# Hybrid attention block on one core: roots, low parts and transposes of the first norm moved, weights of the last norm moved

## Chip, core and metric

The kernel runs on one core of one Trainium2 chip. The core has TensorE (PE in the profile), VectorE (DVE), ScalarE (ACT), GpSimd (POOL) and the SyncE queue (SP), which here issues all transfers. The metric is the device time of one launch in microseconds.

## What is computed

The input x is 1024 x 1024 in float32. With `rms(v, g) = v * rsqrt(mean(v*v) + 1e-6) * g` the block is

```python
h = rms(x, pre_norm_mix)
proj = h @ w_in                        # 1024 x 3280
o_a = sparse_attention(proj, ...)      # scores, top 256 keys of each row, softmax over latents
o_b = gated_delta_rule(proj, ...)      # convolution, chunks of 64, triangular inverses
x = x + rms(concat(o_a, o_b) @ w_out, post_norm_mix)
h = rms(x, pre_norm_mlp)
y = square(relu(h @ w_mlp_in)) @ w_mlp_out
out = x + rms(y, post_norm_mlp)
```

Only the first norm (top line) and the last one (bottom line) are touched by the change, and the first loads of `w_in`.

## The kernel before

Large products are made from split operands: a float32 matrix is written as a high part, rounded to fp32r, and a low part, the difference. `mm3` (L199 to L201) then issues three matmuls: high x high, low x high, high x low.

**Start.** 34 matmuls on zeros run on PE while the eight 128-row tiles of x are loaded. The rows are worked on in two halves of four tiles. For each half ScalarE squares the tiles and sums them (L312), VectorE makes the factor 1/sqrt of four columns in `rsqrt` (L313, then by shifting the bits of the number and three refining steps of three instructions, L212 to L217) and scales the four tiles (L317). Then come eight blocks k of 128 columns: PE transposes four 128 x 128 pieces into one PSUM bank (L321), ScalarE writes the high part `hTH` with the norm's weight as scale (L323), VectorE the low part `hTL` (L324). The bank comes from `pst()`, a pool `tr` of two banks. `psx()` hands out banks of `tr` and of a second pool of two, `ch`, in turn.

**Columns of w_in.** `fetch(i)` loads the i-th group of columns of `plan` into `stg`, ScalarE (for i under 7) or GpSimd casts it to the high part `wh` (L266, L268), and GpSimd subtracts for the low part `wl` (L269). Group 0 has 80 columns (keys of the indexer, gates), groups 1 to 4 have 128 (queries of the indexer). The products go into a PSUM tile `two` that holds both halves of the rows; the second half of group 0 is written only when VectorE has read the first half (L383 to L385).

**Middle.** Scores of the indexer (L471 to L479), a bitwise search for the 256th largest score on VectorE and ScalarE (L521 to L533), convolutions (L587 to L592), chunked recurrences, attention, output product and the two MLP products.

**End.** For each of eight row blocks PE adds a last stretch of w_mlp_out to two banks (24 matmuls), VectorE adds the banks to the sum in SBUF (L1776), and `finish` makes the last norm: ScalarE squares and sums (L1272), VectorE and ScalarE make the factor (`rsqrt` with `act=True`: L209 is a square root from ScalarE's table, L210 its reciprocal, and L215 to L217 one refining step), GpSimd multiplies the sum by the norm's weights (L1763, two halves of 512 columns), VectorE multiplies by the factor and adds x (L1764), SyncE stores.

The order of instructions on each engine is set when the program is built: a scheduler with its own cost model merges the streams. Each engine then works off its list in that order and waits on semaphores.

Of the kernel before, what the change touches and what calls it, by code (L numbers as in the profile page):

```python
# [8 lines left out]
F32 = mybir.dt.float32  # L9
# [4 lines left out]
OP = mybir.AluOpType  # L14
# [125 lines left out]
def block_kernel(ctx: ExitStack, tc: tile.TileContext, x, w_in, c_norm, w_uk, w_uv, rel_bias, conv_w, a_log,  # L140
# [4 lines left out]
    V, S, G, PE, SY = nc.vector, nc.scalar, nc.gpsimd, nc.tensor, nc.sync  # L145
# [4 lines left out]
    w_in, c_norm, w_uk, w_uv, conv_w, a_log = w_in[0], c_norm[0], w_uk[0], w_uv[0], conv_w[0], a_log[0]  # L150
# [22 lines left out]
    def psw():  # L173
        return pl.t(ps_w, [P, T], F32, "two")

    def pst():
        return pl.t(ps_t, [P, 512], F32, "tr")

    def psc():
        return pl.t(ps_c, [P, 512], F32, "ch")  # L180

    def pss():
        return pl.t(ps_s, [P, 512], F32, "sc")
# [3 lines left out]
    def psx():  # L187

        turns[0] += 1
        return (pst, psc)[turns[0] % 2]()  # L190
# [12 lines left out]
    def rsqrt(pool, a, n, tag, y=None, act=False):  # L203


        y = pl.t(pool, [P, n], F32, tag + "_y", bufs=4) if y is None else y
        u = pl.t(pool, [P, n], F32, tag + "_u", bufs=4)
        if act:
            S.activation(y, a, AF.Sqrt)  # L209
            V.reciprocal(y, y)  # L210
        else:
            V.tensor_scalar(u.bitcast(I32), a.bitcast(I32), 1, None, op0=OP.logical_shift_right)  # L212
            V.tensor_scalar(y.bitcast(I32), u.bitcast(I32), -1.0, float(0x5F3759DF), op0=OP.mult, op1=OP.add)
        for _ in range(1 if act else 3):
            V.scalar_tensor_tensor(u, y, -0.5, y, op0=OP.mult, op1=OP.mult)  # L215
            V.tensor_mul(u, u, a)
            V.scalar_tensor_tensor(y, u, 1.5, y, op0=OP.add, op1=OP.mult)  # L217
        return y

    def paired(t):  # L220

        return t.rearrange("p (b a) -> p a b", a=2)

    def halves(t):
        return t.rearrange("p (a b) -> p a b", a=2)
# [26 lines left out]
    hTH = pl.t(hp_, [P, NK, T], F32R, "hTH")  # L252
    hTL = pl.t(hp_, [P, NK, T], F32R, "hTL")

    def load_cols(cols, w=w_in, act=True, stage=None):

        n = sum(c for _, c in cols)
        wh = pl.t(wp, [P, NK, P], F32R, "wh")
        wl = pl.t(wp, [P, NK, P], F32R, "wl")
        f = pl.t(stage, [P, NK, P], F32, "stg", bufs=2) if stage else pl.t(stg, [P, NK, P], F32, "stg")  # L260
        at = 0
        for c0, c in cols:
            SY.dma_start(f[:, :, at:at + c], w[:, c0:c0 + c].rearrange("(k p) c -> p k c", p=P))
            at += c
        if act:
            S.copy(wh[:, :, :n], f[:, :, :n])  # L266
        else:
            G.tensor_scalar(wh[:, :, :n], f[:, :, :n], 1.0, 1.0, op0=OP.mult, op1=OP.mult)  # L268
        G.tensor_sub(wl[:, :, :n], f[:, :, :n], wh[:, :, :n].bitcast(F32))  # L269
        return wh, wl, n  # L270

    plan = [("kw", 0)] + [("qi", p) for p in range(4)] + [(n, h) for h in range(4) for n in ("kb", "qb")]
# [2 lines left out]
    loaded = {}  # L275

    def fetch(i):
        if i < len(plan) and i not in loaded:
            kind, p = plan[i]
            cols = [(C_KI, 72), (C_AB, 8)] if kind == "kw" else [(first[kind] + P * p, P)]  # L280
            loaded[i] = load_cols(cols, act=i < 7)

    kq, kq_close = pl.open("kq", side="right")
    px, px_close = pl.open("px", side="right")
# [3 lines left out]
    ps = psw()  # L288
# [3 lines left out]
    for tb in range(NB):  # L292
        xt = pl.t(px, [P, D], F32, f"x{tb}")
        r0 = tb // 4 * 512 + tb % 2 * 256 + tb % 4 // 2
        SY.dma_start(xt, x[r0:r0 + 255:2, :])
        xs.append(xt)
        if tb == 3:
            sv = pl.t(px, [66, P], F32, "sv")
            SY.dma_start(sv[0:48, :], conv_w.rearrange("j (b p) -> (j b) p", p=P))
            SY.dma_start(sv[48:56, :], pre_norm_mix.rearrange("(k p) -> k p", p=P))  # L300
            SY.dma_start(sv[56:57, :], o_norm[None, :])
            SY.dma_start(sv[57:65, :], pre_norm_mlp.rearrange("(k p) -> k p", p=P))
            fetch(0)
    ps = pst()
# [3 lines left out]
    for half in range(2):  # L308
        ss = pl.t(px, [P, 4], F32, f"ss{half}")
        for j in range(4):  # L310
            junk = pl.t(px, [P, D], F32, "junk", bufs=2)
            S.activation(junk, xs[half * 4 + j], AF.Square, accum_out=ss[:, j:j + 1])  # L312
        V.tensor_scalar(ss, ss, 1.0 / D, EPS, op0=OP.mult, op1=OP.add)  # L313
        rs = rsqrt(px, ss, 4, f"rs{half}")
        for j in range(4):
            xt = xs[half * 4 + j]
            V.tensor_scalar(xt, xt, rs[:, j:j + 1], None, op0=OP.mult)  # L317
        for k in range(NK):
            ps = pst()
            for j in range(4):  # L320
                PE.transpose(ps[:, j * P:(j + 1) * P], xs[half * 4 + j][:, k * P:(k + 1) * P], ident)  # L321
            sl = slice(half * 512, half * 512 + 512)
            S.activation(hTH[:, k, sl], ps, AF.Identity, scale=svT[:, 48 + k:49 + k])  # L323
            V.scalar_tensor_tensor(hTL[:, k, sl], ps, svT[:, 48 + k:49 + k], hTH[:, k, sl].bitcast(F32),  # L324
                                   op0=OP.mult, op1=OP.subtract)
# [626 lines left out]
    def projections():  # L952
        nonlocal dna, dn, dn_close
        for i, (kind, p) in enumerate(plan):
            for j in range(1, 3):
                fetch(i + j)
# [293 lines left out]
    gain = c_row.rearrange("p n c -> p (n c)")  # L1250
    r2 = pl.t(keep, [P, NB], F32, "r2")
    pool, wo, h2, early = {}, [], {}, []
# [14 lines left out]
    def sumsq(ps, pool, out=None, bufs=3, act=False):  # L1267

        s2 = pl.t(pool, [P, 2], F32, "s2", bufs=4)
        for c in range(2):  # L1270
            junk = pl.t(pool, [P, 512], BF16, "jk", bufs=bufs)
            S.activation(junk, ps[c], AF.Square, accum_out=s2[:, c:c + 1])  # L1272
        v = pl.t(pool, [P, 1], F32, "v", bufs=4)
        V.tensor_scalar(v, s2[:, 0:1], s2[:, 1:2], 1.0 / D, op0=OP.add, op1=OP.mult)
        V.tensor_scalar(v, v, EPS, None, op0=OP.add)
        return rsqrt(pool, v, 1, "rm", out, act)
# [90 lines left out]
    stage, x1 = {}, {}  # L1367
# [96 lines left out]
    def tmp(dtype=F32):  # L1464
        return pl.t(tmpp, [P, 512], dtype, "tmp2")
# [109 lines left out]
    while ready:  # L1575
# [4 lines left out]
        ps = bank_[{2: 1, 3: 5, 4: 7}.get(j, j)]  # L1580
# [138 lines left out]
    while ready:  # L1719
# [4 lines left out]
        c, j, ops = ready.pop(0)  # L1724
# [3 lines left out]
        for t in range(4):  # L1728
            ps = bank_[set_][t]
# [11 lines left out]
    for f in range(NS):  # L1741
# [5 lines left out]
        w = []  # L1747
# [5 lines left out]
    def finish(tb, yt):  # L1753
        xr = pl.t(stg, [P, D], F32, "stg")

        r0 = tb // 4 * 512 + tb % 4 * 64
        for a in range(2):
            SY.dma_start(xr[a::2, :], x1_d[r0 + 256 * a:r0 + 256 * a + 64, :])
        r = sumsq(yt, fin, bufs=1, act=True)
        for c in range(2):  # L1760
            cs = slice(c * 512, c * 512 + 512)
            yg = tmp()
            G.tensor_tensor(halves(yg), paired(yt[c]), halves(gain[:, cs]), OP.mult)  # L1763
            V.scalar_tensor_tensor(xr[:, cs], yg, r, xr[:, cs], op0=OP.mult, op1=OP.add)  # L1764
            for a in range(2):
                SY.dma_start(out[r0 + 256 * a:r0 + 256 * a + 64, cs], xr[a::2, cs])


    for tb in range(NB):
        yt = [acc[n][:, tb % 4] for n in (("11", "12"), ("21", "22"))[tb // 4]]  # L1770
        for c in range(2):
            ps = psc() if c else pss()
            for f, (hq, w) in enumerate(rows):
                ts_ = slice(tb * P, (tb + 1) * P)
                mm3(ps, hq[:, 0, ts_], hq[:, 1, ts_], w[c][0], w[c][1], f == 0, f == NS - 1, True)
            V.tensor_add(yt[c], yt[c], ps)  # L1776
        finish(tb, yt)
# [28 lines left out]
```

## Time and profile before

| | |
|---|---|
| runs (us) | 1382.74, 1387.98, 5743.25; median 1387.98 |
| profiled execution | 1387.9 us, of which the span from first to last instruction is 1386.2 |
| granted TensorE clock, mean | 0.965 of full |
| busy share of the span | PE 93%, DVE 80%, ACT 53%, POOL 18% |

The profile counts an engine as busy while it executes; a row of the timeline has its start, its duration, the instruction and, in brackets, how long the engine sat idle before it and what it waited for.

### The profile page before, as it was taken

The page shows a single profiled execution, that of the slowest core. Times are in us where ns is not written, and L with a number is a line of the kernel's source. Part 1 is how long each engine was busy: PE and PEld are TensorE (multiplying, and loading weights), DVE is VectorE, ACT ScalarE, POOL GpSimd, SP SyncE. Part 2 cuts the span into 40 slices and gives each one's busy share as a digit, 9 for nine tenths or more (in the row PEclk, how much of TensorE's full clock was granted, in tenths as well). Part 3 has the DMA queues.
Part 4 walks back from the last instruction along what each step waited for, and adds up shares of the span by engine and source line. Part 5 has one row for each costly group of instructions (what it writes and reads, how often), then busy time and mean ns, then how long its engine had stood idle before and what let it go on. Part 6 is the DMA issues. An engine that isn't in the chain of part 4 may idle for free.

```text
span 1386.2 us, 20222 instructions
## 1 busy us (share of the span) xinstructions
PE 1284.0 (93%) x6628; PEld 1110.4 (80%) x6628; DVE 1108.2 (80%) x2552; ACT 735.4 (53%) x1543; POOL 253.7 (18%) x276
## 2 busy tenths in 40 slices
PE   7899999888777999998989899999999899999995
PEld 4578888777666999877878788888887788888885
DVE  5555779999998888987677467888777987888886
ACT  5455457676624777776455456566666333333422
POOL 3112322122233444348020000000000000000023
PEclk8999999999987999999999899999999999999998
DMA  6223224445055332324355916655566975746215
GB/s 195 66 88 106 61 77 122 137 140 134 23 142 155 97 114 81 93 86 162 125 180 185 298 67 213 213 204 196 208 213 239 392 259 203 251 120 206 77 52 176
DMA packets 184146, 213.33 MB, mean 154 GB/s; under 512 B 28161, under 2 KB 123626, under 8 KB 183914
## 3 DMA queue, kind: packets, MB, share of 16 engines
q1 hardware_dynamic: 184042, 212.06, 47.2%
q8 instruction: 52, 0.85, 0.2%
q14 instruction: 52, 0.43, 0.1%
HBM read 138.58 MB, written 75.00 MB: 154 GB/s over the span
## 4 chain that ended last, share of the span: by engine, by line
PE 65%; DVE 19%; DMA 7%; ACT 5%; issue 2%; POOL 0%; SPq 0%; DVEq 0%; ACTq 0%
PE sc L199 4%; PE sc L200 4%; PE sc L201 4%; PE ch L201 4%; PE ch L199 4%; PE ch L200 4%; PE acc L199 4%; PE acc L200 4%; PE acc L201 4%; DVE pre L528 3%; PE two L199 3%; PE two L200 3%; PE two L201 3%; PE tr L199 2%; PE tr L201 2%
## 5 line engine op out<-in xcount | busy, mean ns | idle before, releaser
L199 PE MATMUL two<-hTH,wh 128*128 128x512 f32 (+1 forms) x416 | 164.5, 398 | 23.0 <-ACT tmp L409 10.6
L200 PE MATMUL two<-hTL,wh 128*128 128x512 f32 (+1 forms) x416 | 163.9, 394 | 0.0
L201 PE MATMUL two<-hTH,wl 128*128 128x512 f32 (+1 forms) x416 | 162.0, 391 | 0.0
L1763 POOL TENSOR_TENSOR tmp<-acc,c_row 128x512 f32<-128x512 f32 x16 | 20.7, 1301 | 644.1 <-DVE acc L1776 632.5
L521 ACT ACTIVATE jk<-score,cand 128x1024 bf16<-128x1024 f32 (+2 forms) x96 | 92.4, 964 | 46.8 <-DVE cand L533 36.2
L199 PEld LDWEIGHTS two<-hTH,wh 128*128 128x128 f32 (+1 forms) x416 | 80.6, 194 | 38.9 <-issue 19.7
L200 PEld LDWEIGHTS two<-hTL,wh 128*128 128x128 f32 (+1 forms) x416 | 80.8, 194 | 11.7 <-issue 0.5
L201 PEld LDWEIGHTS two<-hTH,wl 128*128 128x128 f32 (+1 forms) x416 | 80.1, 193 | 12.0 <-issue 0.5
L1426 ACT CAST hl<-raw 128x512 fp32r<-128x512 f32 x81 | 48.6, 614 | 71.4 <-PE acc L200 51.5
L269 POOL TENSOR_TENSOR wl<-stg,wh 128x1024 fp32r<-128x1024 f32 (+1 forms) x26 | 61.1, 2351 | 80.7 <-ACT wh L266 79.3
L1426 ACT CAST hl<-tt 128x512 fp32r<-128x512 f32 x56 | 34.4, 616 | 72.9 <-PE tr L200 44.6
L1426 ACT CAST hl<-tmp 128x512 fp32r<-128x512 f32 x60 | 35.8, 617 | 55.9 <-DVE tmp L1543 30.6
L1427 DVE TENSOR_TENSOR hl<-raw,hl 128x512 fp32r<-128x512 f32 x81 | 55.2, 684 | 4.5 <-ACT hl L1426 3.3
L1187 ACT CAST part<-tr 128x512 fp32r<-128x512 f32 x80 | 42.7, 542 | 27.3 <-PE tr L1185 24.0
L1162 ACT ACTIVATE big<-big,nm 128x256 f32<-128x256 f32 (+6 forms) x64 | 50.4, 789 | 11.3 <-DVE nm L1161 9.4
L1188 DVE TENSOR_TENSOR part<-tr,part 128x512 fp32r<-128x512 f32 x80 | 50.0, 629 | 4.3 <-ACT part L1187 4.0
L1210 PE MATMUL acc<-part,VS 128*128 128x256 f32 x288 | 51.7, 303 | 0.7 <-DVE part L1188 0.7
L268 POOL TENSOR_SCALAR wh<-stg 128x1024 fp32r<-128x1024 f32 x19 | 19.9, 1049 | 174.8 <-PE two L200 160.6
L589 DVE SCALAR_TENSOR_TENSOR tmp<-two,svT,tmp 128x1023 f32<-128x1023 f32 (+2 forms) x36 | 45.9, 1276 | 6.1 <-ACT tmp L587 6.0
L1138 POOL TENSOR_TENSOR mt<-tz,maskb 128x256 f32<-128x256 f32 x56 | 37.6, 681 | 59.3 <-DVE mx L1154 46.2
L199 PE MATMUL acc<-h2H,hl 128*128 128x512 f32 x120 | 46.3, 387 | 1.6 <-ACT tmp L1477 1.6
L1185 PE MATMUL tr<-ident,big 128*128 128x128 f32 x288 | 46.7, 277 | 0.5 <-DVE part L1188 0.4
(507 smaller groups left out, 4121.7 us busy)
## 6 DMA issues: line engine op xcount, KB each, us to landing
hid<-tmp SPq DMA_DIRECT2D x140, 256.0 KB, 2.6
hq<-hid SPq DMA_DIRECT2D x80, 256.0 KB, 5.3
raw<-in_w_mlp_in_dram SPq DMA_DIRECT2D x14, 1024.0 KB, 5.5
tmp<-hid SPq DMA_DIRECT2D x56, 256.0 KB, 5.4
raw<-in_w_mlp_out_dram SPq DMA_DIRECT2D x13, 1024.0 KB, 7.4
stg<-in_w_in_dram SPq DMA_DIRECT2D x25, 512.0 KB, 4.3
x<-in_x_dram SPq DMA_DIRECT2D x8, 512.0 KB, 5.3
la_d<-la SPq DMA_DIRECT2D x8, 512.0 KB
```

What stands on the lines that cost most here:

```text
L199: PE.matmul(o, lh, rh, start=start, stop=False, skip_group_check=more)
L200: PE.matmul(o, lh, rl, start=False, stop=False, skip_group_check=more)
L201: PE.matmul(o, ll, rh, start=False, stop=stop, skip_group_check=more)
L269: G.tensor_sub(wl[:, :, :n], f[:, :, :n], wh[:, :, :n].bitcast(F32))
L521: S.activation(junk[:, :n], s_of(b), AF.Sign, bias=cand[:, 3 + i:4 + i].bitcast(F32), scale=-1.0, accum_out=cnt[:, 3 + i:4 + i])
L589: V.scalar_tensor_tensor(acc[:, 3 - j:T], both[:, 0:T - 3 + j], w[j], acc[:, 3 - j:T], op0=OP.mult, op1=OP.add)
L1162: S.activation(pr[:, :n], pr[:, :n], AF.Exp, bias=nm, accum_out=den[:, hh:hh + 1])
L1185: PE.transpose(ps[:, c * P:(c + 1) * P], u["p"][hh][:, (j + a) * P:(j + a + 1) * P], ident)
L1188: V.tensor_sub(pt[:, 0:2 * nj, 1, :], v4(ps)[:, 0:2 * nj], pt[:, 0:2 * nj, 0, :].bitcast(F32))
L1210: PE.matmul(po[:, hh * 256:hh * 256 + 256], VS[:, j + a, 2 * p + hh, :], pt[:, 2 * a + hh].rearrange("p a t -> p (a t)"), start=j + a + hh ...
L1426: S.copy(h_, src)
L1427: eng.tensor_sub(l_, src, h_.bitcast(F32))
```

## The change

Four edits:

- `rsqrt` of the first norm is called with `act=True`: square root from ScalarE's table, reciprocal and one refining step on VectorE, in place of the bit shift and three steps on VectorE.
- The low parts `wl` of column groups 0, 1 and 2 are subtracted on VectorE (`early`), those of the others still on GpSimd.
- The transposes of h use `psx()`, four banks in turn, in place of two.
- The weights of the last norm (L1763) are multiplied on VectorE in place of GpSimd.

```diff
@@ load_cols
-    def load_cols(cols, w=w_in, act=True, stage=None):
+    def load_cols(cols, w=w_in, act=True, stage=None, early=False):
...
-        G.tensor_sub(wl[:, :, :n], f[:, :, :n], wh[:, :, :n].bitcast(F32))
+        (V if early else G).tensor_sub(wl[:, :, :n], f[:, :, :n], wh[:, :, :n].bitcast(F32))
@@ fetch
-            loaded[i] = load_cols(cols, act=i < 7)
+            loaded[i] = load_cols(cols, act=i < 7, early=i < 3)
@@ first norm
-        rs = rsqrt(px, ss, 4, f"rs{half}")
+        rs = rsqrt(px, ss, 4, f"rs{half}", act=True)
...
-            ps = pst()
+            ps = psx()
@@ finish
-            G.tensor_tensor(halves(yg), paired(yt[c]), halves(gain[:, cs]), OP.mult)
+            V.tensor_tensor(halves(yg), paired(yt[c]), halves(gain[:, cs]), OP.mult)
```

What that does to the order. First ScalarE, from the squares of the second half on (`junk` is the square that is thrown away, `ss` its sum, `ab` a gate's parameter, `wh` the high parts of groups 1 and 2, `tr` and `ch` the PSUM banks). Before:

```order
L312 ACTIVATE junk_271,ss_40_266<-x_22_176 128x1024
L323 ACTIVATE hTH_107<-tr_210,svT_76 128x512
L323 ACTIVATE hTH_107<-tr_217,svT_76 128x512
L312 ACTIVATE junk_273,ss_40_266<-x_23_178 128x1024
L643 ACTIVATE ab_77_382<-ab_77_382 128x4
L266 CAST wh_385<-stg_387 128x1024
L323 ACTIVATE hTH_107<-tr_224,svT_76 128x512
L266 CAST wh_391<-stg_393 128x1024
L323 ACTIVATE hTH_107<-tr_231,svT_76 128x512
```

Now (the first four `hTH` stand ahead of these rows):

```order
L312 ACTIVATE junk_265,ss_40_260<-x_22_176 128x1024
L312 ACTIVATE junk_267,ss_40_260<-x_23_178 128x1024
L643 ACT_TABLE_LOAD
L643 ACTIVATE ab_77_370<-ab_77_370 128x4
L323 ACTIVATE hTH_107<-ch_232,svT_76 128x512
L323 ACTIVATE hTH_107<-tr_239,svT_76 128x512
L266 CAST wh_373<-stg_375 128x1024
L323 ACTIVATE hTH_107<-ch_246,svT_76 128x512
L209 ACT_TABLE_LOAD
L209 ACTIVATE rs_y_270<-ss_40_260 128x4
L266 CAST wh_379<-stg_381 128x1024
L323 ACTIVATE hTH_107<-tr_253,svT_76 128x512
```

The root of the second half stands behind both squares, two table loads, three high parts and a cast; a first table load and root stand behind the first four squares, and a fourth new load ahead of L626.

Next VectorE at the factor of the second half (`rs_u`, `rs_y`: its two work columns). Before:

```order
L215 SCALAR_TENSOR_TENSOR rs_u_277<-rs_y_276 128x4
L216 TENSOR_TENSOR rs_u_277<-rs_u_277,ss_40_266 128x4
L324 SCALAR_TENSOR_TENSOR hTL_108<-tr_224,svT_76,hTH_107 128x512
L217 SCALAR_TENSOR_TENSOR rs_y_276<-rs_u_277,rs_y_276 128x4
L215 SCALAR_TENSOR_TENSOR rs_u_277<-rs_y_276 128x4
L216 TENSOR_TENSOR rs_u_277<-rs_u_277,ss_40_266 128x4
L217 SCALAR_TENSOR_TENSOR rs_y_276<-rs_u_277,rs_y_276 128x4
L324 SCALAR_TENSOR_TENSOR hTL_108<-tr_231,svT_76,hTH_107 128x512
L317 TENSOR_SCALAR x_20_172<-x_20_172,rs_y_276 128x1024
```

Now:

```order
L313 TENSOR_SCALAR ss_40_260<-ss_40_260 128x4
L324 SCALAR_TENSOR_TENSOR hTL_108<-ch_232,svT_76,hTH_107 128x512
L324 SCALAR_TENSOR_TENSOR hTL_108<-tr_239,svT_76,hTH_107 128x512
L269 TENSOR_TENSOR wl_374<-stg_375,wh_373 128x1024
L324 SCALAR_TENSOR_TENSOR hTL_108<-ch_246,svT_76,hTH_107 128x512
L210 RECIPROCAL rs_y_270<-rs_y_270 128x4
L269 TENSOR_TENSOR wl_380<-stg_381,wh_379 128x1024
L215 SCALAR_TENSOR_TENSOR rs_u_271<-rs_y_270 128x4
L324 SCALAR_TENSOR_TENSOR hTL_108<-tr_253,svT_76,hTH_107 128x512
L216 TENSOR_TENSOR rs_u_271<-rs_u_271,ss_40_260 128x4
L217 SCALAR_TENSOR_TENSOR rs_y_270<-rs_u_271,rs_y_270 128x4
L317 TENSOR_SCALAR x_20_172<-x_20_172,rs_y_270 128x1024
```

All eight low parts `hTL` of the first half, and two low parts of weights, now stand ahead of the scaling of the second half; before, four `hTL` did.

Last VectorE in the last two row blocks. Before:

```order
L1764 SCALAR_TENSOR_TENSOR stg_14033<-tmp_3180_14056,rm_y_14044,stg_14033 128x512
L1776 TENSOR_TENSOR acc_2548_11331<-acc_2548_11331,ch_14075 128x512
L1274 TENSOR_SCALAR v_14097<-s_3184_14092 128x1
L1275 TENSOR_SCALAR v_14097<-v_14097 128x1
L210 RECIPROCAL rm_y_14100<-rm_y_14100 128x1
L215 SCALAR_TENSOR_TENSOR rm_u_14101<-rm_y_14100 128x1
L216 TENSOR_TENSOR rm_u_14101<-rm_u_14101,v_14097 128x1
L217 SCALAR_TENSOR_TENSOR rm_y_14100<-rm_u_14101,rm_y_14100 128x1
L1764 SCALAR_TENSOR_TENSOR stg_14089<-tmp_3190_14107,rm_y_14100,stg_14089 128x512
L1764 SCALAR_TENSOR_TENSOR stg_14089<-tmp_3191_14112,rm_y_14100,stg_14089 128x512
```

Now:

```order
L1776 TENSOR_TENSOR acc_2548_11319<-acc_2548_11319,ch_14063 128x512
L1764 SCALAR_TENSOR_TENSOR stg_14021<-tmp_3179_14039,rm_y_14032,stg_14021 128x512
L1764 SCALAR_TENSOR_TENSOR stg_14021<-tmp_3180_14044,rm_y_14032,stg_14021 128x512
L1763 TENSOR_TENSOR tmp_3191_14100<-acc_2548_11319,c_row_339 128x512
L1274 TENSOR_SCALAR v_14085<-s_3184_14080 128x1
L1275 TENSOR_SCALAR v_14085<-v_14085 128x1
L210 RECIPROCAL rm_y_14088<-rm_y_14088 128x1
L215 SCALAR_TENSOR_TENSOR rm_u_14089<-rm_y_14088 128x1
L216 TENSOR_TENSOR rm_u_14089<-rm_u_14089,v_14085 128x1
L217 SCALAR_TENSOR_TENSOR rm_y_14088<-rm_u_14089,rm_y_14088 128x1
L1764 SCALAR_TENSOR_TENSOR stg_14077<-tmp_3190_14095,rm_y_14088,stg_14077 128x512
L1764 SCALAR_TENSOR_TENSOR stg_14077<-tmp_3191_14100,rm_y_14088,stg_14077 128x512
```

The last bank's sum (L1776) now stands ahead of the output of the block before it (L1764), and the two products L1763 of each block stand between the sums and the factor.

## Rows read from the trace of the kernel before

**Rows 1.** The page: span, and an engine's busy time, share and instructions.

```profile
span 1386.2 us, 20222 instructions
PE 1284.0 (93%) x6628; PEld 1110.4 (80%) x6628; DVE 1108.2 (80%) x2552; ACT 735.4 (53%) x1543; POOL 253.7 (18%) x276
```

**Rows 2.** Stretches: length, busy (instructions) of PE, PEld, DVE, ACT, POOL, clock, DMA.

```profile
48.00:52.00 4.00, 4.00 (x10) 2.47 (x11) 2.30 (x4) 0.59 (x1) 0.00 (x0) 0.50 0.00 0
...
200.00:425.00 225.00, 191.83 (x880) 163.40 (x879) 217.56 (x547) 134.98 (x277) 58.19 (x36) 0.92 0.42 117
```

**Rows 3.** Timeline of VectorE, 8 to 48 us: start, duration, instruction, idle before.

```profile
10.97 0.17 DVE L313 TENSOR_SCALAR ss<-ss 128x4 f32<-128x4 f32 x1 [9.77 <-ACT junk L312]
...
12.18 1.38 DVE L215 SCALAR_TENSOR_TENSOR rs_u<-rs_y 128x4 f32<-128x4 f32 x1
...
14.59 2.74 DVE L317 TENSOR_SCALAR x<-x,rs_y 128x1024 f32<-128x1024 f32 x4
...
21.44 2.24 DVE L215 SCALAR_TENSOR_TENSOR rs_u<-rs_y 128x4 f32<-128x4 f32 x1
...
27.88 2.75 DVE L317 TENSOR_SCALAR x<-x,rs_y 128x1024 f32<-128x1024 f32 x4
...
42.39 0.75 DVE L324 SCALAR_TENSOR_TENSOR hTL<-tr,svT,hTH 128x512 fp32r<-128x512 f32 x1 [0.17 <-ACT hTH L323]
...
44.61 0.75 DVE L324 SCALAR_TENSOR_TENSOR hTL<-tr,svT,hTH 128x512 fp32r<-128x512 f32 x1 [0.16 <-ACT hTH L323]
...
47.06 0.69 DVE L385 COPY tmp<-two 16x512 f32<-16x512 f32 x1
```

**Rows 4.** Timeline of GpSimd, 8 to 48 us.

```profile
12.00 1.54 POOL L269 TENSOR_TENSOR wl<-stg,wh 128x640 fp32r<-128x640 f32 x1 [7.73 <-ACT wh L266]
21.30 4.66 POOL L269 TENSOR_TENSOR wl<-stg,wh 128x1024 fp32r<-128x1024 f32 x2 [7.76 <-ACT wh L266]
```

**Rows 5.** Timeline of ScalarE, 8 to 48 us.

```profile
17.89 1.27 ACT L323 ACTIVATE hTH<-tr,svT 128x512 fp32r<-128x512 f32 x2
19.05 1.06 ACT L312 ACTIVATE junk<-x 128x1024 f32<-128x1024 f32 x1
```

**Rows 6.** Timeline of PE: transposes in the first half, restart for the second.

```profile
19.42 1.11 PE L321 MATMUL tr<-ident,x 128*128 128x128 f32 x4
...
47.89 0.69 PE L199 MATMUL two<-hTH,wh 128*80 128x512 f32 x1 [4.04 <-DVE tmp L385]
```

**Rows 7.** Timeline of ScalarE, 50 to 70 us, with a table load.

```profile
65.49 0.23 ACT L632 ACTIVATE y<-y 128x32 f32<-128x32 f32 x1 [2.14 <-DVE y L631]
...
66.83 1.28 ACT L635 ACT_TABLE_LOAD   x1
68.12 0.23 ACT L635 ACTIVATE w<-w 128x32 f32<-128x32 f32 x1
```

**Rows 8.** Groups by line and shape: a subtraction of 1024 columns on VectorE.

```profile
L1746 DVE TENSOR_TENSOR raw<-stg,raw 128x1024 fp32r<-128x1024 f32 x4 | 4.8, 1220 | 2.1 <-ACT raw L1745 2.1
```

**Rows 9.** Groups: the product with a norm's weights on VectorE and on GpSimd.

```profile
L1353 DVE TENSOR_TENSOR yg<-ch,c_row 128x512 f32<-128x512 f32 x10 | 6.9, 686 | 4.3 <-ACT jk L1272 4.2
...
L1763 POOL TENSOR_TENSOR tmp<-acc,c_row 128x512 f32<-128x512 f32 x16 | 20.7, 1301 | 644.1 <-DVE acc L1776 632.5 <-issue 5.4 <-DVE rm_y L210 2.3
```

**Rows 10.** Timeline of PE: its last two matmuls.

```profile
1371.20 0.38 PE L200 MATMUL ch<-hq,raw 128*128 128x512 f32 x1
1371.42 0.38 PE L201 MATMUL ch<-hq,raw 128*128 128x512 f32 x1
```

**Rows 11.** Timeline of VectorE after PE's end.

```profile
1376.09 1.41 DVE L1764 SCALAR_TENSOR_TENSOR stg<-tmp,rm_y,stg 128x512 f32<-128x512 f32 x2 [0.23 <-DVE rm_y L217]
1377.42 0.68 DVE L1776 TENSOR_TENSOR acc<-acc,ch 128x512 f32<-128x512 f32 x1
...
1380.59 1.41 DVE L1764 SCALAR_TENSOR_TENSOR stg<-tmp,rm_y,stg 128x512 f32<-128x512 f32 x2 [0.22 <-DMA out_dram<-stg]
```

**Rows 12.** Groups of VectorE, 200 to 425 us: a step of the search on six columns.

```profile
L531 DVE TENSOR_SCALAR bare<-cand 128x6 int32<-128x6 int32 x31 | 10.7, 345 | 0.0
```

## The prediction

> **What bounds the kernel now.** I read the page first: PE is busy for 1284.0 of 1386.2 us [rows 1], so over most of the span only PE work or waits of PE count, and this change removes no matmul. Then the stretches: from 200 to 425 us VectorE is busy for 217.6 of 225 us [rows 2], so there VectorE is the bound, and what comes earlier into that stretch also leaves it earlier. Then the two ends, where the edits lie, instruction by instruction. At the start PE depends on the norm: it begins the second half of the rows at 47.89, after 4.04 us of idling for the copy L385 [rows 6], which is the end of this chain: squares, factor, scaling (L317), transposes, high parts, low parts, three reads of the product. At the end PE finishes at 1371.42 + 0.38 = 1371.8 [rows 10] but VectorE at 1380.59 + 1.41 = 1382.0 [rows 11]: 10.2 us of the norm behind the last matmul, then the stores. Both ends are on the path; if the start is shorter by s and the end by e, I expect s + e.
>
> **Start, first half.** The sums are ready at 10.97 + 0.17 [rows 3]. A table load takes 1.28 [rows 7] and waits for no data, so ScalarE runs it behind the last square, from about 10.95 to 12.2; the root is as small as the 0.23 us activation [rows 7], 0.2; reciprocal and three steps follow at 0.2 each (0.17 and a gap [rows 3]): 13.3, where scaling began at 14.59 [rows 3]. Gain 1.3. Nearly all of it is one stall: L215 took 1.38 at 12.18 [rows 3] in place of 0.17, while GpSimd subtracted low parts from 12.00 to 13.54 [rows 4]. The two edits meet here: the shorter factor pays for the table load, the moved low part removes the stall.
>
> Scaling 2.7 gives 16.0. Before, the first high part came 0.6 after scaling (17.33 to 17.89 [rows 3, 5]): 16.6. With four banks four high parts run without a break at 0.64 each [rows 5], to 19.1; low parts on VectorE follow at 0.75 [rows 3]. The moved subtraction of 80 columns per block (640 elements) fits on VectorE between scaling and the first high part, at two thirds of 1.22 [rows 8], 0.8.
>
> **Start, second half.** Here the new order costs. ScalarE, in its order: two squares at 1.2 with their read-out (1.06 [rows 5]), 21.5; table load 1.28, 22.8; the small exponential, 23.0; two high parts, 24.3; cast of 1024 columns, priced as the square of as many, 1.06 [rows 5], 25.4; high part, 26.1; table load, 27.4; root, 27.6; cast, 28.7. VectorE: the low part of group 2 waits for that cast, 1.22 [rows 8], 29.9; one step, 30.1; the eighth low part 0.75, 30.9; two steps, 31.3; scaling 2.75, 34.0. Before, scaling began at 27.88 and ended at 30.6 [rows 3]: 3.4 later now, although the stalls of VectorE behind GpSimd (L215 took 2.24 at 21.44 [rows 3], during the two subtractions of rows 4, and a second one like it) are gone.
>
> What comes after the scaling is quicker. Before, two banks made a cycle of 2.22 us per two blocks (low parts at 42.39 and 44.61 [rows 3]), because transposes, high part and low part of one bank follow each other. With four banks the low parts set the pace, 0.75 per block: eight take 6.0. So PE restarts at H + 0.7 + 6.0 + 0.1 + 2.1 + 0.15 = H + 9.05, H being the start of the first high part of this half, 2.1 the three reads of 0.69 [rows 3], and 0.15 the gap from L385's end to PE [rows 3, 6].
>
> H is at least 34.0 + 0.5 = 34.5. PE may be later: it has 27 matmuls of groups 0 and 1 to do from 26.7 (the low part of group 1), ahead of these transposes. At full clock they take 27 x 0.22 [rows 10] = 5.9 and are hidden; at the lower level, granted clock 0.50 (1.2 GHz), ten took 4.00 us [rows 2], so 27 take 10.8, and 13 transposes at 0.28 (four in 1.11 [rows 6]) 3.6: H = 41.3. PE waits more from 20 to 26 than before, so I expect the lower level at first, for about 4 us as after the restart [rows 2]: 26.7 + 4.0 + 17 x 0.22 = 34.4, and the 13 transposes at half of 0.28 give H near 36.2. Between 34.5 and 36.2 I take 35.5. PE restarts at 44.55 instead of 47.89: **s = 3.3**, with ends +4.3 (H = 34.5) and -2.5 (H = 41.3).
>
> **The fourth table load** stands ahead of L626, around 63 us. ScalarE idled 2.14 us there for VectorE [rows 7], more than 1.28: nothing. Without that cover it would cost its 1.28.
>
> **End.** L1763 takes 1301 on GpSimd; on VectorE the same product from the other norm takes 686 ns [rows 9]. Its sum operand lies in SBUF here, not PSUM; I take 0.69. VectorE's work per row block becomes: two sums at 0.68, two outputs 1.41 [rows 11], two products 1.37, and six small instructions at 0.2: 5.35, less some overlap (a pair of 1.41 begun at 1376.09 is followed at 1377.42 [rows 11]), about 5.2. PE needs 24 x 0.22 [rows 10] = 5.2. VectorE just keeps up. Behind PE's end then stand: last sum 0.6, outputs of the block before 1.4, product 0.7, two sums of squares 0.4, root and its hand-overs 0.45, four steps 0.8, outputs 1.4: 5.8, where it is 10.2 now. Today the last sum is added only at 1377.42 [rows 11], 5.6 after the bank was full, since it stands behind the previous block's whole factor. **e = 4.4**, with ends 0 (VectorE falls behind by all of it) and 5.
>
> **Sum.** The profiled execution took 1387.9 (span 1386.2 and 1.7 around it), and the median of the runs is 1387.98, so the base is the same. 1387.9 - 3.3 - 4.4 = **1380**.
>
> **Table loads against the trace.** The load in the middle costs 1.28 and no more: the next activation starts at 68.12, 0.01 after the load's end, and no idle time stands before the load [rows 7].
>
> The Trainium skill, on the page "ScalarE: Activation LUTs" (section "What ACT_TABLE_LOAD costs"), speaks against the edit: it counts about 1.38 us of draining on top of each 1283 ns load, 2.66 us per switch. By it the three loads on this path would cost 3 x 1.38 = 4.1 more, and the sum would be 1384. This trace agrees with the 1283 and shows no drain.
>
> **Rivals.** *The switches cost twice* (chance 0.19). Each change of table holds ScalarE for a second 1.28 because its pipeline must empty between dense high parts, where the row above had only small work around it. Three on the path: 3.9, which eats s: 1387.9 + 0.6 - 4.4 = 1384. For it: ScalarE is dense there now. Against it: rows 7. A lasting lower clock of PE (s = -2.5) would give 1387.9 + 2.5 - 4.4 = 1386.
>
> *VectorE and GpSimd collide anew* (0.14), and the kernel gets slower. In the stretch where VectorE is the bound, a step on six columns averages 345 ns, 31 times [rows 12], against 0.17 for its like [rows 3]: 5.4 us of stalls behind GpSimd in that line alone. A full stall costs 2.24 - 0.17 = 2.1 [rows 3]. The scheduler has moved many rows between 60 and 425 us by a few places, so these meetings are dealt again. The point of decision is four more full stalls: 8.4 exceeds s + e = 7.7, and the time is 1389. For it: nothing here keeps them apart. Against: as many may vanish.
>
> *Fewer collisions, or H early and VectorE ahead at the end* (0.20): s = 4.3, e = 5, and one or two stalls less: 1387.9 - 9.3 - 4 = 1374 to 1375.
>
> **Numbers.** The forecast (1376 to 1384) has 0.47. The range takes in the rivals up to five stalls either way: 1370 to 1390. Two per cent is 28 us, about what a measurement of this kernel can tell from no change; 28 us of gain would need ten stalls to vanish beside s and e, 28 of loss seventeen new ones: 0.02 and 0.02.
>
> **What would show it.** In the profile after: scaling of the first half (L317) near 13.3; of the second near 31; low parts of the second half every 0.75; PE's restart near 44.5; no idle ScalarE after a table load; L1763 on VectorE at 0.69; VectorE's end 5.8 behind PE's. Wrong would be a restart of PE at 47 or later, VectorE ending 8 or more behind PE, or a span from 60 us to PE's end that differs by more than 5 us.

## The result and the profile after

The changed kernel takes 1377.5 us (median of 6 runs, 1372.21 to 1379.91), the kernel before 1387.6 beside it: ratio 0.9921, 95% interval 0.9897 to 0.9945. Its profiled execution, the slowest of the six, took 1379.9 (span 1378.2), 8.0 less than that of before. Of these 8.0, the last matmul ends 5.9 us earlier (1365.50 + 0.38 against 1371.8), and VectorE ends 8.1 us behind it instead of 10.2.

ScalarE at the start, the timeline from 8 to 43 us (start, duration, instruction, idle before):

```profile
10.92 1.28 ACT L209 ACT_TABLE_LOAD   x1
12.22 0.20 ACT L209 ACTIVATE rs_y<-ss 128x4 f32<-128x4 f32 x1
...
17.16 0.68 ACT L323 ACTIVATE hTH<-tr,svT 128x512 fp32r<-128x512 f32 x1
17.73 0.69 ACT L323 ACTIVATE hTH<-ch,svT 128x512 fp32r<-128x512 f32 x1
...
21.08 1.28 ACT L643 ACT_TABLE_LOAD   x1
22.37 0.20 ACT L643 ACTIVATE ab<-ab 128x4 f32<-128x4 f32 x1
...
25.27 1.28 ACT L209 ACT_TABLE_LOAD   x1
26.57 0.20 ACT L209 ACTIVATE rs_y<-ss 128x4 f32<-128x4 f32 x1
...
33.53 0.69 ACT L323 ACTIVATE hTH<-ch,svT 128x512 fp32r<-128x512 f32 x1 [5.24 <-PE ch L321]
```

Behind each of the three table loads the next activation starts 1.29 or 1.30 after the load's start. A high part lasts 0.69 in its row, but the next one starts 0.57 later: rows of neighbours overlap by 0.1.

The fourth new load, answering to [rows 7] (timeline of ScalarE, 44 to 72 us):

```profile
56.64 1.28 ACT L626 ACT_TABLE_LOAD   x1
57.93 0.23 ACT L626 ACTIVATE sm_beta<-wab 128x32 f32<-128x32 f32 x1
58.88 0.23 ACT L632 ACTIVATE y<-y 128x32 f32<-128x32 f32 x1 [0.72 <-DVE y L631]
```

VectorE in the same stretch, answering to [rows 3]; then PE, answering to [rows 6]:

```profile
13.26 2.74 DVE L317 TENSOR_SCALAR x<-x,rs_y 128x1024 f32<-128x1024 f32 x4
...
27.74 1.22 DVE L269 TENSOR_TENSOR wl<-stg,wh 128x1024 fp32r<-128x1024 f32 x1 [0.76 <-ACT wh L266]
...
30.00 2.74 DVE L317 TENSOR_SCALAR x<-x,rs_y 128x1024 f32<-128x1024 f32 x4
...
34.92 0.74 DVE L324 SCALAR_TENSOR_TENSOR hTL<-tr,svT,hTH 128x512 fp32r<-128x512 f32 x1
35.58 0.74 DVE L324 SCALAR_TENSOR_TENSOR hTL<-ch,svT,hTH 128x512 fp32r<-128x512 f32 x1
...
40.93 0.68 DVE L385 COPY tmp<-two 16x512 f32<-16x512 f32 x1
```

```profile
41.76 0.69 PE L199 MATMUL two<-hTH,wh 128*80 128x512 f32 x1 [4.07 <-DVE tmp L385]
```

PE restarts 6.1 us earlier than at 47.89. The same stretches by busy time and granted clock (columns as in [rows 2]): PE worked off the first half's backlog at full clock, and the lower level came only with the restart.

```profile
26.00:32.00 6.00, 6.00 (x28) 5.03 (x29) 4.95 (x11) 2.28 (x4) 0.00 (x0) 1.00 0.63 167
41.70:44.60 2.90, 2.84 (x7) 1.85 (x8) 2.47 (x4) 0.59 (x1) 0.00 (x0) 0.50 0.00 0
200.00:425.00 225.00, 188.34 (x851) 158.00 (x849) 215.99 (x541) 131.80 (x271) 59.91 (x37) 0.91 0.42 114
```

VectorE at the end, answering to [rows 11], and the groups of the two products ([rows 9]: busy us, mean ns, idle before):

```profile
1367.65 1.41 DVE L1764 SCALAR_TENSOR_TENSOR stg<-tmp,rm_y,stg 128x512 f32<-128x512 f32 x2 [0.45 <-DVE acc L1776]
1368.98 0.68 DVE L1763 TENSOR_TENSOR tmp<-acc,c_row 128x512 f32<-128x512 f32 x1
...
1372.55 1.41 DVE L1764 SCALAR_TENSOR_TENSOR stg<-tmp,rm_y,stg 128x512 f32<-128x512 f32 x2 [1.56 <-DMA stg<-x_d]
```

```profile
L1763 DVE TENSOR_TENSOR tmp<-acc,c_row 128x512 f32<-128x512 f32 x16 | 13.2, 828 | 0.1
L1764 DVE SCALAR_TENSOR_TENSOR stg<-tmp,rm_y,stg 128x512 f32<-128x512 f32 x16 | 11.3, 746 | 2.5 <-DMA stg<-x_d 1.8 <-DVE acc L1776 0.7
```

The last outputs wait 1.56 us for their rows of x (L1758). The transfer queue shows why they are late:

```profile
1363.30 1.12 SPq L1758 DMA_DIRECT2D stg<-x_d  x2
1364.84 2.43 SPq L1766 DMA_DIRECT2D out_dram<-stg  x4
1368.86 1.12 SPq L1758 DMA_DIRECT2D stg<-x_d  x2
1370.09 5.63 SPq L1766 DMA_DIRECT2D out_dram<-stg  x8
```

The last load goes into a buffer whose stores (issued from 1364.84 to 1367.27) must land first; it is issued at 1368.86, and the stores of the block before stand behind it in the same queue. VectorE waited for x in the kernel before too, at an earlier block; its next output shows the 0.22 that also stands ahead of the last one in [rows 11]:

```profile
1365.44 1.42 DVE L1764 SCALAR_TENSOR_TENSOR stg<-tmp,rm_y,stg 128x512 f32<-128x512 f32 x2 [1.55 <-DMA stg<-x_d]
...
1370.78 1.41 DVE L1764 SCALAR_TENSOR_TENSOR stg<-tmp,rm_y,stg 128x512 f32<-128x512 f32 x2 [0.22 <-DVE rm_y L217]
```

### The profile page after: what moved, and what is told of

It reads as the page before. It is cut to its first block, busy times and chain, and to the rows that moved or that the text cites. A ratio compares the mean times of both kernels' runs of the same rounds, so it can differ in the third digit from the quotient of the medians.

```text
span 1378.2 us, 20181 instructions
## 1 busy us (share of the span) xinstructions
PE 1280.1 (93%) x6628; PEld 1107.6 (80%) x6628; DVE 1111.6 (81%) x2557; ACT 738.0 (54%) x1549; POOL 226.1 (16%) x257
## 4 chain that ended last, share of the span: by engine, by line
PE 66%; DVE 21%; DMA 5%; ACT 4%; issue 2%; SPq 1%; DVEq 0%; ACTq 0%
PE sc L199 4%; PE acc L199 4%; PE sc L200 4%; PE acc L200 4%; PE sc L201 4%; PE acc L201 4%; PE ch L199 4%; PE ch L200 4%; PE ch L201 4%; PE two L199 3%; PE two L200 3%; PE two L201 3%; DVE pre L528 3%; PE tr L199 2%; PE tr L200 2%
## 5 line engine op out<-in xcount | busy, mean ns | idle before, releaser
L199 PE MATMUL two<-hTH,wh 128*128 128x512 f32 (+1 forms) x416 | 166.0, 400 | 22.7 <-ACT tmp L409 14.3
L199 PEld LDWEIGHTS two<-hTH,wh 128*128 128x128 f32 (+1 forms) x416 | 80.7, 194 | 39.3 <-issue 18.8
L269 POOL TENSOR_TENSOR wl<-stg,wh 128x1024 fp32r<-128x1024 f32 x23 | 54.7, 2376 | 81.1 <-ACT wh L266 63.7
L199 PE MATMUL acc<-h2H,hl 128*128 128x512 f32 x120 | 46.6, 390 | 3.9 <-ACT tmp L1477 3.9
L479 DVE SCALAR_TENSOR_TENSOR score<-ch,wab,score 128x512 f32<-128x512 f32 (+3 forms) x40 | 26.0, 655 | 28.1 <-ACT ch L478 27.8
```

The costliest lines, as they stand in the source:

```text
L199: PE.matmul(o, lh, rh, start=start, stop=False, skip_group_check=more)
L269: (V if early else G).tensor_sub(wl[:, :, :n], f[:, :, :n], wh[:, :, :n].bitcast(F32))
```

## The experiments

Twelve kernels ran, each beside runs of the kernel before on the same chip (medians 1388.6 for 1 to 4, 1389.3 for 5 to 8, 1390.1 for 9 to 12). The table has them all; single entries are explained below. **Restart**: PE's L199 after L385. **Tail**: VectorE's end behind PE's end. **Order**: PE's matmuls of the middle as in the kernel before (old) or in the changed one (new). In the traces, from the 2001st to the 5600th matmul that is not on zeros (some 470 to 1157 us in the kernel before), the five old lists agree row for row, the nine new ones differ in at most 5 rows, and between the two kinds some 1200 of the 3600 rows differ. The lists of VectorE and ScalarE differ between the kinds as well, so "order" means that of the whole program. **Stretch**: from PE's 3000th to its 3500th instruction, some 585 to 667 us, the same set of instructions in both orders. **Rest**: (1 - ratio) x median of before, less the restart's gain on 47.89, less the tail's gain on 10.2; it is what the two ends don't explain, in us. It carries the uncertainty of the ratio, some 3 us either way, and that of one trace: the tail alone varies from 7.6 to 9.6 between seven kernels with the same code at the end (the changed one and 1, 2, 3, 5, 9, 10).

| kernel | ratio (95%) | restart | tail | order | stretch | rest |
|---|---|---|---|---|---|---|
| before | 1 | 47.89 | 10.2 | old | 86.9 | |
| changed | 0.9921 (0.9897-0.9945) | 41.76 | 8.1 | new | 82.3 | 2.7 |
| 1 root by bits | 0.9961 (0.9939-0.9982) | 40.88 | 9.6 | old | 88.9 | -2.2 |
| 2 low parts on GpSimd | 0.9960 (0.9940-0.9981) | 44.55 | 8.0 | old | 83.2 | 0.0 |
| 3 two banks | 0.9977 (0.9956-0.9997) | 47.16 | 9.4 | old | 84.4 | 1.7 |
| 4 product on GpSimd | 0.9922 (0.9895-0.9949) | 41.84 | 10.1 | new | 79.3 | 4.7 |
| 5 bits, two low parts | 0.9921 (0.9898-0.9944) | 42.48 | 7.6 | new | 78.6 | 3.0 |
| 6 x in spare tiles | 0.9872 (0.9853-0.9891) | 41.72 | 5.4 | new | 82.1 | 6.8 |
| 7 before + four banks | 0.9944 (0.9922-0.9966) | 44.00 | 11.2 | new | 78.7 | 4.9 |
| 8 = 5 with 6 | 0.9906 (0.9887-0.9925) | 41.73 | 5.4 | new | 79.5 | 2.1 |
| 9 35 zero matmuls | 0.9932 (0.9909-0.9954) | 42.23 | 8.5 | old | 81.8 | 2.1 |
| 10 33 zero matmuls | 0.9900 (0.9875-0.9924) | 42.31 | 7.7 | new | 78.7 | 5.8 |
| 11 = 6, product on GpSimd | 0.9905 (0.9873-0.9938) | 41.82 | 7.25 | new | 78.5 | 4.2 |
| 12 before + one low part | 0.9975 (0.9956-0.9994) | 47.20 | 10.5 | new | 79.6 | 3.1 |

**1, the root by bits again.**

```diff
-        rs = rsqrt(px, ss, 4, f"rs{half}", act=True)
+        rs = rsqrt(px, ss, 4, f"rs{half}")
```

> The first norm's root by bits again (1/sqrt by shift and three steps on VectorE), the other three edits kept. Theory A: the start gained by the low parts on VectorE (no stall behind GpSimd) and by the four banks, while the root costs time in the second half, where its two table loads hold ScalarE between the high parts. Then nothing of the gain is lost: PE restarts (L199 after L385) at 38.5 to 41, 1 to 3 us before the changed kernel's 41.76, and the time is 1 to 3 us lower than the changed kernel's. Theory B: the shorter factor is a real part of the gain: restart at 43 or later, time up by 1.3 us or more. Scaling of the first half: 14.0 under both (13.26 with the root), as the steps without a stall take 0.17 to 0.2 each.

The restart came at 40.88, 0.9 us earlier than with the root: as far as the restart goes the root is a small loss, so theory B falls. But theory A fails too in its time: this kernel is slower than the changed one, by 0.4% of the ratio. In its profiled execution (1387.8, which is 6.0 above its median) the 7.0 us of the start were lost behind the restart; by the ratio, which gives a gain of 5.4, 2.2 us of start and tail were. That led to runs 5, 9 and 10.

**2, the low parts on GpSimd again.**

```diff
-        (V if early else G).tensor_sub(...)
+        G.tensor_sub(...)
```

> The first three low parts back on GpSimd, the other three edits kept. Theory A (stalls of VectorE behind GpSimd were what the move removed): an instruction of VectorE beside the subtractions on GpSimd takes 1.3 to 2.3 us again in place of 0.2 to 0.75, and PE restarts 1 to 4 us later than 41.76, at 43 to 46. Rival (the move only shifted 3.3 us of subtraction from GpSimd to VectorE, which is the busier engine): restart earlier, at 38.5 to 41.

44.55, 2.8 us later. VectorE's scaling of four tiles takes 3.93 and 4.63 beside the subtractions instead of 2.74 (timelines of VectorE and of GpSimd):

```profile
13.27 3.93 DVE L317 TENSOR_SCALAR x<-x,rs_y 128x1024 f32<-128x1024 f32 x4
...
30.21 4.63 DVE L317 TENSOR_SCALAR x<-x,rs_y 128x1024 f32<-128x1024 f32 x4
```

```profile
13.12 1.54 POOL L269 TENSOR_TENSOR wl<-stg,wh 128x640 fp32r<-128x640 f32 x1 [8.85 <-ACT wh L266]
...
29.00 2.36 POOL L269 TENSOR_TENSOR wl<-stg,wh 128x1024 fp32r<-128x1024 f32 x1 [0.69 <-ACT wh L266]
...
31.50 0.73 POOL L447 MEMSET tmp<- 32x768 f32 x1
```

The subtractions still ran when the scaling was due: for 13.12 + 1.54 - 13.27 = 1.4 us, with a loss of 1.19, and for 29.00 + 2.36 - 30.21 = 1.15, with a loss of 1.89. Each loss falls almost wholly on the first of the four scalings (groups of VectorE, 13.3 to 15 and 30.9 to 32.6 us; the others take 0.74 to 0.80):

```profile
L317 DVE TENSOR_SCALAR x<-x,rs_y 128x1024 f32<-128x1024 f32 x1 | 1.9, 1944 | 0.0
L317 DVE TENSOR_SCALAR x<-x,rs_y 128x1024 f32<-128x1024 f32 x1 | 2.6, 2564 | 0.0
```

They end at 15.21 and 32.77, each 0.5 to 0.6 behind a row of GpSimd: the first behind the subtraction (14.66), the second behind the memset L447 (32.23). So the memset may have lengthened the second stall; no run separates the two. The stall theory holds.

**3, two banks again** (`ps = pst()`).

> Transposes of h in two banks again, the other three edits kept. Theory A (the bank cycle set the pace): eight blocks of the second half take 8 x 1.11 in place of 8 x 0.66, so PE restarts 3.6 us later, at 45.4; the first half loses up to 3 us more if its low parts come late for the second half's scaling, so 45 to 48. Rival (ScalarE's high parts set the pace anyway, at 0.64 each): restart within 1 us of 41.76.

47.16, in theory A's range, and the low parts of the second half stand in the old cycle, a step of 0.9 and one of 1.3 in turn:

```profile
38.98 0.75 DVE L324 SCALAR_TENSOR_TENSOR hTL<-tr,svT,hTH 128x512 fp32r<-128x512 f32 x1 [0.17 <-ACT hTH L323]
40.28 0.75 DVE L324 SCALAR_TENSOR_TENSOR hTL<-tr,svT,hTH 128x512 fp32r<-128x512 f32 x1 [0.55 <-ACT hTH L323]
41.20 0.75 DVE L324 SCALAR_TENSOR_TENSOR hTL<-tr,svT,hTH 128x512 fp32r<-128x512 f32 x1 [0.17 <-ACT hTH L323]
```

Of the start's 6.1 us the banks are worth 5.4. The undone edits give 5.4 (banks), 2.8 (low parts) and -0.9 (root); their sum is 7.3 and not 6.1, so they are not independent: added alone to the kernel before, the banks bring 3.9 (kernel 7).

**4, the last norm's product on GpSimd again** (L1763: `V` to `G`).

> The last norm's weights multiplied on GpSimd again, the other three edits kept. Both theories leave the start as it is (restart 41.8). Theory A (the move shortened the end by 2.1 us): VectorE ends 10.2 us behind PE's end, the time is 2.1 us above the changed kernel's. Rival (the end is set by the stores and the load of x on the transfer queue, whichever engine multiplies): VectorE ends 8 us behind PE's end, no difference.

The tail is 10.1 as expected, but the ratio is that of the changed kernel (0.9922). Intervals of about 0.25% either way (3.5 us) hide 2 us, so the time settles nothing here; only the tail in the profile speaks, for theory A.

**5, the root by bits and only two low parts on VectorE** (edit 1, and `early=i < 3` to `i < 2`).

> As the kernel with the root by bits, but only the low parts of groups 0 and 1 on VectorE, that of group 2 on GpSimd. Its start is nearly that kernel's (restart there 40.88). What differs: the scheduler's order of PE's instructions between 400 and 900 us is, but for 3 rows, that of the changed kernel, while the kernel with the root by bits had there the order of the kernel before. Theory C (the changed kernel gained 3 to 5 us in the middle because the scheduler came out with another order there): restart 40.5 to 43, time 3 to 5 us below that of the kernel with the root by bits: 0.991 to 0.993 of before. Rival (the order makes no difference; that kernel was slow because of something in its start): time within 1.5 us of its 0.9961.

0.9921 against 0.9961 of kernel 1, although it restarts 1.6 us later. This is as theory C has it; the two intervals just overlap.

**6, x in spare tiles**: every second block's rows of x are loaded into two spare tiles, in four pieces of 64 x 512.

```diff
-        xr = pl.t(stg, [P, D], F32, "stg")
...
+        if tb % 2:
+            xc = [pl.t(rooms["tt"], [P, 512], F32, "tt") for _ in range(2)]
...
+        else:
+            xr = pl.t(stg, [P, D], F32, "stg")
+            xc = [xr[:, 0:512], xr[:, 512:1024]]
```

> The changed kernel, with the rows of x for the last norm of every second row block loaded into spare 128x512 tiles, so that a block's load doesn't wait until the stores of two blocks before have landed. Start and middle as in the changed kernel. Theory D (the missing 2 us of the end are the wait of the last output for its rows of x, 1.56 us, held up on the transfer queue): that wait is gone and VectorE ends 5.8 to 6.5 us behind PE's end in place of 8.1; time 1.5 to 2 us lower. Rival (the products on VectorE are longer than priced and VectorE falls behind by itself): 7.5 to 8.1.

The tail is 5.4, and the last outputs follow the factor without a wait:

```profile
1363.23 0.16 DVE L217 SCALAR_TENSOR_TENSOR rm_y<-rm_u,rm_y 128x1 f32<-128x1 f32 x1
1363.43 1.41 DVE L1771 SCALAR_TENSOR_TENSOR tt<-tmp,rm_y,tt 128x512 f32<-128x512 f32 x2
```

Theory D holds. At 1370.8 us (1367.18 to 1374.71) this kernel beats the changed one; by the ratios the difference is 6.8 us, where 1.5 to 2 were expected. Only 2.7 us of it are the tail, and the rest is not explained. In the two profiles 4.7 us lie between PE's 867th and 1700th instruction (211.8 against 216.6), which over all kernels took from 211.8 to 217.1.

**7, the kernel before with four banks alone** (`ps = psx()`).

> The kernel before with one edit, transposes of h in four banks. PE's order in the middle is that of the changed kernel but for 3 rows. Banks alone: the second half's eight blocks at 0.66 to 0.75 in place of 1.11 bring 3 us, restart 44 to 45.5 (47.89 before); stalls behind GpSimd stay. Theory C: 3 from the start and 3 to 5 from the order, 0.994 to 0.996 of before. Rival (order without effect): 3 us, 0.998.

Restart 44.00, 3.9 us earlier, and the ratio lies in theory C's range.

**8, kernels 5 and 6 together.**

> The root by bits, two low parts on VectorE, four banks, the last norm's product on VectorE and the rows of x in spare tiles together, with the changed kernel's order in the middle. Theories C and D: start 0.5 to 1 us and end 1.5 to 2 us better than the changed kernel, 0.989 to 0.991 of before, 1374 to 1376. Rivals: as the changed kernel or worse, 0.992 and up.

Within the forecast by the ratio, yet not better than kernel 6 (1375.5 against 1370.8), with the same restart and tail; the start is not the 0.5 to 1 us better that was expected. So the rest differs by some us between kernels of one order, which a median of five or six runs doesn't resolve.

**9 and 10, one more and one fewer matmul on zeros**: `range(34)` to 35 and to 33. All four edits stay, but the order of the middle is the old one with 35 and the new one with 33.

> The changed kernel with 35 matmuls on zeros at the very start instead of 34 (0.26 us of PE, before x has arrived). All four edits stay; but the scheduler now comes out with the kernel before's order of PE's instructions in the middle. Theory C (the other order is worth 3 to 6 us between 580 and 680 us): restart as in the changed kernel, 41.7 to 42.1, and the time 3 to 6 us above that with 33, 0.995 to 0.997 of before; PE's instructions 3000 to 3500 take 83 to 89 us. Rival (the order is without effect; the kernels' other differences made it): within 1.5 us of the one with 33.

> The changed kernel with 33 matmuls on zeros at the start instead of 34; the scheduler keeps the changed kernel's order in the middle. The control of the run with 35: as the changed kernel under both theories, 0.991 to 0.993 of before, restart 41.5 to 42; PE's instructions 3000 to 3500 take 78 to 83 us under theory C.

The restarts are equal (42.23, 42.31), the medians 1379.6 and 1373.4, the ratios 0.9932 and 0.9900, both lower than expected (0.995 to 0.997, 0.991 to 0.993). By the ratios the difference is 4.4 us, within theory C's bounds, but the intervals overlap. The stretch took 81.8 and 78.7, a smaller difference than expected (81.8 is under 83). About half of these 3.1 us is idle time of PE, 7.7 against 6.3. PE's waits in it, first with 35, then with 33 (what waited, what for, us in total, times, longest):

```profile
PE acc L1233 <- DVE ol L1229: 2.7, 2, 1.8
PE ch L199 <- ACT oh L1307: 1.7, 2, 1.0
PE acc L1210 <- DVE part L1188: 1.3, 2, 1.1
PE acc L1238 <- DVE orow L1235: 0.7, 2, 0.5
PE tr L1185 <- DVE part L1188: 0.6, 2, 0.4
...
```

```profile
PE acc L1210 <- DVE part L1188: 2.7, 3, 1.6
PE tr L1185 <- DVE part L1188: 1.8, 3, 1.1
PE ch L199 <- ACT oh L1307: 0.9, 1, 0.9
...
```

In the old order PE waits for the sums that close the attention's last blocks (L1229, L1235); in the new one these waits are gone. In the other kernels of the old order 1.8 to 3.6 us for L1308 come on top, and in kernel 1 and in the kernel before the mean granted clock of the stretch is 0.96 and 0.94 where it is 1.00 with 35 and with 33.

**11, kernel 6 with the product on GpSimd.**

> The changed kernel with the rows of x in spare tiles (VectorE's end 5.4 us behind PE's there), but the last norm's weights multiplied on GpSimd again. Theory (the multiplication on VectorE is worth 4.4 us at the end once the load of x no longer waits): VectorE ends 9.5 to 10.2 us behind PE's end, time 4 to 5 us above that kernel's 0.9872. Rival (VectorE was late for the rows of x in both): 5.5 to 7.

7.25, between the two: neither forecast. By the ratios the time is 4.6 us above kernel 6's, as the theory has it, but the tail accounts for 1.8 of that and the intervals overlap. Of the tail's 10.2 us, then, in these profiles, the load of x takes 2.9 with the product on GpSimd (10.1 to 7.25) and 2.7 with it on VectorE (8.1 to 5.4), and the product 1.8 to 2.0. The load was late in the kernel before as well (the 1.55 us above).

**12, the kernel before with group 0's low part on VectorE** (`early=i < 1`).

> The kernel before with one edit: the low part of group 0 alone (80 columns) on VectorE. The stall of 1.2 us in the first factor goes (0.8 us of subtraction comes), restart 46 to 47.9. PE's order in the middle is, but for 3 rows, the changed kernel's. Theory C: 3 to 6 us from the order and 0 to 1.5 from the start, 0.995 to 0.998 of before, instructions 3000 to 3500 in 78 to 83 us. Rival: 0.999 to 1.000, 83 to 89 us.

0.9975, with a start only 0.7 us earlier: what is left, 3.1 us, is of the size that theory C gives to the order. The stretch, 79.6, is as theory C has it too. But the interval reaches to 0.9994, and so into the rival's range.

**Over all kernels** the rest is 0.4 us on average for the four with the old order (-2.2 to 2.1) and 4.2 for the nine with the new one (2.1 to 6.8); the stretch takes 85.0 on average (with the kernel before) and 79.7. So the order is worth about 3.8 us, with a standard error of 1.1 from the scatter of the kernels. The stretch itself varies by 7 us within the old order, and the clock has a part in that. At a granted clock of 1.00 it took 81.8 to 84.4 us in three kernels of the old order (2, 3, 9) and 78.5 to 79.6 in seven of the new one (4, 5, 7, 8, 10 to 12), without an overlap. The changed kernel and kernel 6 had 0.98 there and took 82.3 and 82.1, so their profiles show the new order at less than its worth.

## Why the prediction came out

The number was right: 1380 forecast, 1379.9 profiled, 1377.5 the median. Its sum was not: two terms were mis-sized in opposite directions, s by +2.8 and e by -2.3, and a third, the order of the middle, was missing. That s + e came to 8.2 where 7.7 was forecast is luck. By two signs that the prediction itself named it was wrong: VectorE ended 8.1 behind PE (8 or more), and from 60 us to PE's end it took 5.9 us less (more than 5), since the larger gain of the start is in that span.

- **First half**: scaling at 13.3 forecast, 13.26 seen; first high part 16.6, 16.57 seen. Right, with its reason: the stall of [rows 3, 4] is gone, and kernel 2 brings such a stall back.
- **Second half, too late by 2.8 us** (s = 3.3 forecast, 6.1 measured, beyond the upper end of 4.3). Scaling came at 30.00 instead of 31.3, since I added durations where starts follow at 0.57 (high parts, taken as 0.64 to 0.7) and 0.94 (casts, 1.06). H, the first high part, was 33.53, under the earliest value. PE cost little: the lower clock for its backlog, for which I had added 1.0, didn't come (1.00 from 26 to 32 us), and H stood 0.8 behind the scaling's end in place of 0.5. The low parts followed at 0.66 and not at 0.75, which makes the last 0.8: 1.3 + 1.0 - 0.3 + 0.8 = 2.8. (The late end, H = 41.3, adds up to 41.1 from its own terms; only a rival uses it.)
- **Table loads**: 1.28 each and no more, three times among dense work. The rival in which the switches cost twice is wrong, and with it the drain of about 1.38 us that the Trainium skill states ("ScalarE: Activation LUTs", "What ACT_TABLE_LOAD costs"); its 1283 ns agree. The fourth load cost nothing, as forecast: it stands in ScalarE's wait for VectorE, which shrank from 2.14 to 0.72. The root still costs 0.9 us of the restart (kernel 1).
- **End, e = 4.4 forecast, 2.1 measured.** The chain behind the last matmul was counted rightly as 5.8: it is 5.4 once nothing else waits (kernel 6). I had left out the load of x (L1758), which the kernel before has at the same place. The last of [rows 11] names a transfer at the last output, but its 0.22 us stands at other outputs too, where it is put down to the factor; what showed the late load was the wait of 1.55 at an earlier block, which the prediction does not mention. L1763 takes 0.83 and not 0.69, but the last one, the only one behind PE's end, takes 0.68, so that the tail doesn't show it.
- **Middle "unchanged"**: right as a sum in the profiled execution (1323.9 and 1324.1 us from the restart to PE's end), wrong as a reason. PE stood 2.7 us ahead of before at its 3000th instruction and 7.3 ahead at its 3500th. The start's gain shrank from 6.4 to 3.0 between its 867th and 1700th instruction, where VectorE is the bound; that loss swings between kernels by some us either way, and I can't lay it to the change. The 585 to 667 us then gave back about as much, 4.6, of which a part may be the granted clock (0.94 before, 0.98 now). Across the kernels the new order is worth about 3.8 us; that would cover the 2.5 us by which the median lies below the forecast, but the intervals are as wide.
- **VectorE and GpSimd collide anew**: by the step of [rows 12] they did so less, though the stretch as a whole lost time. In the 200 to 425 us that step averages 252 ns instead of 345:

```profile
L531 DVE TENSOR_SCALAR bare<-cand 128x6 int32<-128x6 int32 x30 | 7.6, 252 | 0.0
```

Open stays why the rest of kernel 6 is 6.8 and that of kernel 8 only 2.1; why L1763 takes 0.83 beside PE's work; and which of the moved rows makes the new order shorter.

## What to carry to other kernels

Where a scheduler lays out the program, an edit at the start can move hundreds of instructions elsewhere: compare the lists of the whole program, and look for a neutral edit (here one matmul on zeros) that flips the order alone before a gain is put down to the edit itself. Add starts, not durations, where instructions of one engine follow densely. At the end of a kernel, follow a named transfer to the queue that issues it before pricing the arithmetic: in the profiles here the load that no one had meant to change was worth more (2.7 us) than the product that was moved (1.8 to 2.0).

## What the hardware showed that was not expected

- Dense rows of ScalarE and VectorE overlap by about 0.1 us: high parts of 0.69 start every 0.57, low parts of 0.74 every 0.66.
- A subtraction on GpSimd holds up VectorE's scaling, an instruction with one tensor operand: 2.74 became 3.93 and 4.63 (kernel 2), and almost all of the loss is one instruction's each time, 1.94 and 2.56 in place of 0.75. The Trainium skill calls the pair's shared port an exclusive lock ("SBUF — State Buffer", "SBUF: two separate sides"); the first loss, 1.19 against 1.4 of overlap, agrees roughly; the second, 1.89 against 1.15, is longer than the overlap with the subtraction alone.
- In the changed kernel PE kept its full clock through 22 to 26 us, where it was busy for 2.87 of 4; it fell to the lower level after idling 3.84 us behind the zero matmuls, and again at the restart, after 4.07 us of idling: 0.50 from 41.7 to 44.6 (columns as in [rows 2]):

```profile
14.30:17.70 3.40, 3.40 (x17) 2.68 (x15) 2.98 (x6) 2.88 (x6) 0.00 (x0) 0.50 0.99 354
22.00:26.00 4.00, 2.87 (x13) 1.28 (x10) 2.71 (x4) 3.97 (x7) 0.00 (x0) 1.00 0.02 4
```
